# Turned identity transposes, first weights' low parts on GpSimd, and later or earlier low halves in a one-core transformer block

## The chip, the cores and the metric

The kernel runs on one core of one Trainium2 chip. TensorE (PE) multiplies matrices; its weight loads (PEld) run beside the products. VectorE (DVE), ScalarE (ACT) and GpSimd (POOL) do everything else on tiles, and SyncE (SP) issues nearly all transfers. Each engine works through its own instructions in a fixed order and stops at an instruction whose semaphore is not there yet. The metric is the device time of one execution in microseconds, taken as the median over several executions.

## The reference

One layer of a bidirectional hybrid encoder on x of 1024 tokens by 1024 features, in float32. What is computed:

```
h = rmsnorm(x, norm_mix);  proj = h @ w_in      # q k v r, low-rank decays, pool input, two gates
o = gla_forward(q,k,v,decay_f) + gla_backward(q,k,v,decay_b)   # 4 heads, chunked linear attention
y_a = (rmsnorm_per_head(o) * gla_norm * silu(r)) @ w_branch
y_b = (multiscale_pool(u) per group @ w_pool_group) * pool_scale
x = x + (sigmoid(g_a)*y_a + sigmoid(g_b)*y_b) @ w_out
x = x + (silu(gate) * up) @ w_ffn_out,  [gate | up] = rmsnorm(x, norm_ffn) @ w_ffn_in
return rmsnorm(x, norm_final)
```

The chunked attention keeps a state per head: for a chunk, `kv = k^T v`, and the state is `decay * state + kv`; the output of a chunk is a product of masked scores with v and a product of q with the state before the chunk.

## The kernel before

**Products in two halves.** Every float32 operand of a large product is split into a high half, a rounding to fp32r by a cast, mostly on ACT, and a low half, the rest, by a subtraction on DVE or POOL (`split_to`, L197 to L199). Three products take the place of one: high by high, high by low, low by high (`products`, `mm3`). A high half must exist before its low half can be made, so each split is a step of ACT followed by a step of DVE or POOL, and PE can start on the first of the three products before the low halves are there. Large products of the later stages are cut into Strassen-like seven-product schemes, whose sums and differences of blocks (`sub`, `add` on DVE, `padd` on POOL) come ahead of the splits.

**What sets the order.** The program is written out in order by generators. `mm3` calls `pump`, which after a given amount of PE work takes the next step of a side generator (`begin(gen, delay)`), so that transposes, norms and splits are interleaved with the running products. Each engine's order is fixed by that.

**The start** (L446 to L490). Rows of x come in eight tiles of 128 tokens. For each, ACT squares and sums it (`xn<-x`, L331), DVE adds the epsilon (`n1rs`, L322), POOL takes the power -1/2 (L323), DVE scales (`xn`, L327). PE transposes the scaled tile with `ident` (`tr`, L338), two tiles to a bank pair, ACT multiplies by the gain and casts (`hh`, L345), DVE makes the low half (`hl`, L348). PE forms the values of head 0 and the low-rank decays for one tile after the other (`first_values`, 288 columns, t = 0 to 7); their weights `raw` and `lraw` are split into `fwh` and `fwl` (L198, L199, L249, L251). ACT evicts each result (`vh`, `lr`) and DVE makes `vl`.

**A GLA head.** The backward scan runs over chunks 7 to 1. A step multiplies keys and values (`kv`), DVE makes the new state `st` (L764) and its decayed form `so` (L769), and ACT writes the state for later use into `sb` (L815). Between the steps PE transposes keys (`kp`, L750), which ACT and DVE split into `kt`, and forms the scores `sc` (L777), which DVE masks (L782) and which are split into `p`. Then the forward scan forms the output `op`: scores by values, and `sb` by q (L849).

**Merge and output product.** `merged_piece` (L1184) makes the operands of the seven products with `w_out`; for p = 6 it calls `sub`, `padd`, `sub` (L1198 to L1200), and the low half `dl` follows (L163).

**FFN operands.** `features(half)` (L1491) transposes the normalised rows; ACT evicts them into `hb` (L1506), DVE forms sums and differences (L1518, L1522), ACT casts them to `gh` (L1484), DVE makes the low half `gl` (L1488, `low_block`).

## Time and profile before

| | |
|---|---|
| median of 3 runs | 1383.6 us (1383.58 to 1387.52) |
| profiled execution | 1385.57 us |
| its span, first to last instruction | 1383.8 us |
| PE busy | 1362.2 us, 98% |
| DVE, POOL, ACT busy | 848.3, 757.6, 625.1 us |
| mean granted TensorE clock | 0.999 |

The span and the profiled execution's own time differ by 1.8 us, which lie around the span. A product of 512 columns starts every 0.23 us, one of 288 columns about every 0.14 us and one of 256 columns every 0.12 us; the durations of the rows are longer than that since products overlap. PE is busy for nearly the whole span, so the other engines matter where PE waits for them, and the table of waits names those places.

### The profile page before, as it was taken

The page shows a single profiled execution, that of the slowest core. Times are in us where ns is not written, and L with a number is a line of the kernel's source. Part 1 is how long each engine was busy: PE and PEld are TensorE (multiplying, and loading weights), DVE is VectorE, ACT ScalarE, POOL GpSimd, SP SyncE. Part 2 cuts the span into 40 slices and gives each one's busy share as a digit, 9 for nine tenths or more (in the row PEclk, how much of TensorE's full clock was granted, in tenths as well). Part 3 has the DMA queues.
Part 4 walks back from the last instruction along what each step waited for, and adds up shares of the span by engine and source line. Part 5 has one row for each costly group of instructions (what it writes and reads, how often), then busy time and mean ns, then how long its engine had stood idle before and what let it go on. Part 6 is the DMA issues. An engine that isn't in the chain of part 4 may idle for free.

```text
span 1383.8 us, 18503 instructions
## 1 busy us (share of the span) xinstructions
PE 1362.2 (98%) x6654; PEld 1150.9 (83%) x6654; DVE 848.3 (61%) x1073; ACT 625.1 (45%) x1125; POOL 757.6 (55%) x565
## 2 busy tenths in 40 slices
PE   7999999999999999999999999999999999999997
PEld 7889898988888877788888788888888888888886
DVE  6276767766645885587884856555655556343374
ACT  7365655644334444554346533333333334453252
POOL 3260715312398456568665276666666667464354
PEclk9999999999999999999999999999999999999999
DMA  6221322321487669997416355555444447975451
GB/s 193 77 92 44 110 82 87 122 77 46 138 264 238 211 198 310 334 393 257 152 61 240 118 175 175 175 175 175 159 141 141 145 137 267 385 256 216 167 232 73
DMA packets 167452, 243.56 MB, mean 176 GB/s; under 512 B 10904, under 2 KB 97856, under 8 KB 167360
## 3 DMA queue, kind: packets, MB, share of 16 engines
q1 hardware_dynamic: 154368, 215.11, 46.7%
q10 hardware_dynamic: 12992, 27.27, 5.3%
q8 instruction: 52, 0.85, 0.3%
q14 instruction: 40, 0.33, 0.1%
HBM read 164.48 MB, written 77.86 MB: 175 GB/s over the span
## 4 chain that ended last, share of the span: by engine, by line
PE 81%; POOL 5%; issue 4%; DVE 4%; ACT 3%; DMA 2%; ACTq 0%; POOLq 0%; SPq 0%; DVEq 0%
PE ps L291 75%; POOL wl L199 2%; PE op L849 2%; DMA u_out<-uph 1%; PE kv L291 1%; PE sc L777 1%; PE op L291 1%; POOL qe L733 1%; DVE res L1796 1%; POOL wsum L637 1%; PE yb L291 1%; PE tp L1008 1%; DMA u_out<-upl 0%; DMA raw<-in_w_in_dram 0%; DVE ws L1068 0%
## 5 line engine op out<-in xcount | busy, mean ns | idle before, releaser
L199 POOL TENSOR_TENSOR wl<-fs,wh 128x512 fp32r<-128x512 f32 x120 | 166.2, 1389 | 163.9 <-ACT wh L198 139.4
L291 PE MATMUL ps<-gl,wh 128*128 128x512 f32 x616 | 239.8, 389 | 0.9 <-DVE gl L1488 0.9
L291 PE MATMUL ps<-gh,wh 128*128 128x512 f32 x616 | 240.4, 390 | 0.0
L291 PE MATMUL ps<-gh,wl 128*128 128x512 f32 x616 | 239.7, 389 | 0.0
L199 POOL TENSOR_TENSOR wl<-fraw,wh 128x512 fp32r<-128x512 f32 x90 | 130.1, 1445 | 64.3 <-ACT wh L198 59.5
L199 POOL TENSOR_TENSOR wl<-raw,wh 128x512 fp32r<-128x512 f32 x44 | 63.8, 1463 | 159.0 <-ACT wh L198 158.9
L199 POOL TENSOR_TENSOR ol<-gor,oh 128x1024 fp32r<-128x1024 f32 (+1 forms) x42 | 99.8, 2382 | 92.3 <-ACT oh L198 71.8
L291 PE MATMUL ps<-hh,wh 128*128 128x512 f32 x376 | 149.8, 398 | 0.0
L291 PE MATMUL ps<-hh,wl 128*128 128x512 f32 x376 | 146.6, 390 | 0.0
L291 PE MATMUL ps<-hl,wh 128*128 128x512 f32 x376 | 146.5, 390 | 0.0
L291 PEld LDWEIGHTS ps<-gl,wh 128*128 128x128 f32 x616 | 115.7, 188 | 25.1 <-DVE gl L1488 1.3
L291 PEld LDWEIGHTS ps<-gh,wl 128*128 128x128 f32 x616 | 115.6, 188 | 24.0
L291 PEld LDWEIGHTS ps<-gh,wh 128*128 128x128 f32 x616 | 115.7, 188 | 23.6
L291 PE MATMUL ps<-ol,oh 128*128 128x512 f32 x308 | 119.9, 389 | 0.2 <-DVE ol L199 0.2
L291 PE MATMUL ps<-oh,oh 128*128 128x512 f32 x308 | 119.8, 389 | 0.0
L291 PE MATMUL ps<-oh,ol 128*128 128x512 f32 x308 | 119.8, 389 | 0.0
L199 POOL TENSOR_TENSOR wl<-wraw,wh 128x512 fp32r<-128x512 f32 x56 | 91.3, 1659 | 46.0 <-ACT wh L198 46.0
L199 DVE TENSOR_TENSOR ol<-wor,oh 128x1024 fp32r<-128x1024 f32 (+1 forms) x41 | 61.4, 1520 | 49.5 <-ACT oh L198 49.3
L198 ACT CAST wh<-fs 128x512 fp32r<-128x512 f32 x120 | 73.8, 615 | 32.1 <-DVE fs L918 23.8
L291 PEld LDWEIGHTS ps<-hh,wl 128*128 128x128 f32 x376 | 70.6, 188 | 15.0
L291 PEld LDWEIGHTS ps<-hl,wh 128*128 128x128 f32 x376 | 70.7, 188 | 13.2
L291 PEld LDWEIGHTS ps<-hh,wh 128*128 128x128 f32 x376 | 70.7, 188 | 13.2
(262 smaller groups left out, 3176.4 us busy)
## 6 DMA issues: line engine op xcount, KB each, us to landing
fraw<-in_w_ffn_in_dram SPq DMA_DIRECT2D x44, 512.0 KB, 6.2
gor<-g_out SPq DMA_DIRECT2D x35, 512.0 KB, 7.1
raw<-in_w_in_dram SPq DMA_DIRECT2D x48, 256.0 KB, 3.8
g_out<-s SPq DMA_DIRECT2D x44, 256.0 KB, 2.3
fraw<-in_w_in_dram SPq DMA_DIRECT2D x20, 512.0 KB, 4.5
wor<-t_out SPq DMA_DIRECT2D x20, 512.0 KB, 7.6
g_out<-g SPq DMA_DIRECT2D x33, 256.0 KB, 2.6
x<-in_x_dram SPq DMA_DIRECT2D x16, 512.0 KB, 4.3
```

Source lines behind the costliest of these rows:

```text
L198: nc.scalar.copy(hi, src)
L199: eng.tensor_tensor(lo, src, as_f32(hi), op=ALU.subtract)
L291: nc.tensor.matmul(ps, a[i], b[j], start=first and n == 0, stop=last and n == 2, skip_group_check=onto)
L637: op()
L733: nc.gpsimd.tensor_tensor(e_q[:, d, :], e_q[:, d, :], q[:, half, :], op=ALU.mult)
L777: nc.tensor.matmul(sc[d][:, i * CH : (i + 1) * CH], chunk_of(ke, n, d), chunk_of(qe, n, d), start=True, stop=True,)
L849: nc.tensor.matmul(op[:, :DV], a, b, start=False, stop=j == len(terms) - 1)
L1008: nc.tensor.transpose(tp[:, i * P : (i + 1) * P], o_heads[j // 2][half][:, i, (j % 2) * P : (j % 2 + 1) * P], ident[:, :],)
L1796: nc.vector.scalar_tensor_tensor(res[:, COLS[j]], x2[t][:, COLS[j]], rs[:, :], gain_final[:, COLS[j]], op0=ALU.mult, op1=ALU.mult)
```

## The change

The change has seven parts.

1. Before the first rows arrive, PE transposes `ident` 30 times into a bank that is never read (`spin(30)`), and 8 times more between the transposes of the first and the second row tile.
2. The four casts of `lraw` go from POOL to ACT, between the squares of tiles 0 and 1. The four subtractions that make `fwl` from `raw` are all on POOL; two of them were on DVE.
3. In `first_values` for t = 0 the products with low weights of the last four k-tiles come last.
4. The squares of tiles 2 and 3 are both taken before either is scaled. The transposes of these tiles come at the end of the product t = 1 rather than inside it. The square of tile 4 is taken early, its scaling later; the square of tile 5 comes after the evictions of t = 1.
5. In each GLA head the low halves of the first scores `p` and of the keys `kt` of the forward scan's first half are held back until the next state has been made, and the transposes of these keys come one step earlier.
6. `padd` in `merged_piece` becomes `add`, so this sum goes from POOL to DVE.
7. The low blocks of the fifth FFN product are made two transposes after their cast rather than three.

```diff
@@ -241,12 +241,15 @@
             self.todo = tiles
             self.parts = [tuple(slot(F32R, (2, VL), s) for s in ("fwh", "fwl")) for _ in tiles]
 
-        def split_values(self, i, eng):
-            split_to(*(t[:, :, :DV] for t in self.parts[i]), self.todo[i][:, :, :], eng)
+        def split_values(self, i):
+            hi, lo = (t[:, :, :DV] for t in self.parts[i])
+            src = self.todo[i][:, :, :]
+            nc.scalar.copy(hi, src)
+            nc.gpsimd.tensor_tensor(lo, src, as_f32(hi), op=ALU.subtract)
 
         def split_low(self):
             for i, (hi, _) in enumerate(self.parts):
-                nc.gpsimd.tensor_copy(hi[:, :, DV:], self.low[:, 2 * i : 2 * i + 2, :])
+                nc.scalar.copy(hi[:, :, DV:], self.low[:, 2 * i : 2 * i + 2, :])
             for i, (hi, lo) in enumerate(self.parts):
                 nc.gpsimd.tensor_tensor(
                     lo[:, :, DV:], self.low[:, 2 * i : 2 * i + 2, :], as_f32(hi[:, :, DV:]), op=ALU.subtract
@@ -392,13 +395,17 @@
 
     def norm_x(t):
         rs = norm_scale(xt[t % 4][:, :], xn[t % 4], "n1")
-        scale_by(xn[t % 4], xt[t % 4][:, :], rs)
-        if t + 4 < NT:
-            load_x(t + 4)
+
+        def scaled():
+            scale_by(xn[t % 4], xt[t % 4][:, :], rs)
+            if t + 4 < NT:
+                load_x(t + 4)
+
+        return scaled
 
     def norms(t0):
         for t in (t0, t0 + 1):
-            norm_x(t)
+            norm_x(t)()
             yield 2
 
     def values(w, v, t):
@@ -415,8 +422,20 @@
     def first_values(w, v, t):
 
         ps = bank(ps_mm)
-        for kt in range(KT):
-            mm3(ps[:, :VL], tokens(hT(kt, t // 4), t), w(kt), kt == 0, kt == KT - 1)
+        if t:
+            for kt in range(KT):
+                mm3(ps[:, :VL], tokens(hT(kt, t // 4), t), w(kt), kt == 0, kt == KT - 1)
+        else:
+            terms = [(kt, i, 0) for kt in range(KT) for i in range(2)]
+            for kt in range(4):
+                terms.insert(3 * kt + 1, (kt, 0, 1))
+            terms += [(kt, 0, 1) for kt in range(4, KT)]
+            for n, (kt, i, j) in enumerate(terms, 1):
+                nc.tensor.matmul(
+                    ps[:, :VL], tokens(hT(kt, 0), 0)[i], w(kt)[j], start=n == 1, stop=n == len(terms)
+                )
+                if n % 3 == 0:
+                    pump(VL / HALF)
         hi, lo = (part[:, t % 4, :] for part in v[t // 4])
         nc.scalar.copy(hi, ps[:, :DV])
         nc.scalar.copy(low_rows[:, t, :, :], ps[:, DV:VL].unsqueeze(1).broadcast_to([P, 4, 2 * RANK]))
@@ -440,8 +459,16 @@
     def value_slots():
         return [(slot(F32R, (4, DV), "vh"), slot(F32R, (4, DV), "vl")) for _ in range(2)]
 
+    def spin(n):
+        for _ in range(n):
+            nc.tensor.transpose(spun[:, :P], ident[:, :], ident[:, :])
+
+    spun = bank(ps_mm, "spun")
+    spin(30)
     v = value_slots()
-    norm_x(0)
+    norm_x(0)()
+    w = FirstWeights(first_raw, lraw)
+    w.split_low()
 
     vps = bank(ps_g, "vps")
     cols = [const.tile([P, n], F32, tag=f"cols{n}", name=f"cols{n}") for n in (8, n_rows)]
@@ -455,21 +482,35 @@
     g_mix = cols[0]
     g_ffn, g_gla, g_pool = (cols[1][:, 8 * i : 8 * i + 8] for i in range(3))
     b_dec = (cols[1][:, 24:28], cols[1][:, 28:32])
-    norm_x(1)
+    norm_x(1)()
     trs = [bank(ps_g, "tr") for _ in range(KT // 2)]
     for t in range(2):
         for kp, ps in enumerate(trs):
             transpose_tile(ps, xn[t], t, kp)
-    w = FirstWeights(first_raw, lraw)
-    w.split_low()
+        if t == 0:
+            spin(8)
     for i in range(KT // 2):
-        w.split_values(i, nc.vector if i < 2 else nc.gpsimd)
+        w.split_values(i)
     for kp, ps in enumerate(trs):
         gain_and_split(ps, kp, 0, hT, g_mix)
-    norm_x(2)
-    norm_x(3)
+    for scaled in [norm_x(t) for t in (2, 3)]:
+        scaled()
+    fifth = []
+
+    def fifth_mean():
+        fifth.append(norm_x(4))
+        yield 1
+
+    def fifth_and_sixth():
+        fifth.pop()()
+        yield 0.1
+        norm_x(5)()
+        yield 0.1
+
     for t in range(0, NT, 2):
-        if t + 4 < NT:
+        if t == 0:
+            begin(fifth_mean(), 1)
+        elif t + 4 < NT:
             begin(norms(t + 4), 1)
         if t == 2:
             for d, w_up in enumerate((w_decay_up_fwd, w_decay_up_bwd)):
@@ -481,7 +522,9 @@
         if t == 0:
             vectors(1, 8)
         if t + 2 < NT:
-            begin(to_features(xn[(t + 2) % 4 :], t + 2, hT, g_mix, 1 if t else 0.6), 0.5 if t else 2.2)
+            begin(to_features(xn[(t + 2) % 4 :], t + 2, hT, g_mix, 1 if t else 0.15), 0.5 if t else 3.9)
+        if t == 0:
+            begin(fifth_and_sixth())
         first_values(w, v, t + 1)
         finish_side()
         if t == 4:
@@ -744,12 +787,20 @@
         def chunk_of(e, n, d):
             return e[n // 4][:, d, (n % 4) * CH : (n % 4 + 1) * CH]
 
-        def transposed_keys(half, d):
+        def split_with(lows, hi, lo, src):
+            nc.scalar.copy(hi, src)
+            low = partial(nc.vector.tensor_tensor, lo, src, as_f32(hi), op=ALU.subtract)
+            if lows is None:
+                low()
+            else:
+                lows.append(low)
+
+        def transposed_keys(half, d, lows=None):
             kp = bank(ps_g, "kp")
             for i in range(4):
                 nc.tensor.transpose(kp[:, i * P : (i + 1) * P], chunk_of(ke, 4 * half + i, d), ident[:, :])
             kt = slot(F32R, s="kt")
-            split_to(kt[:, 0, :], kt[:, 1, :], kp[:, :])
+            split_with(lows, kt[:, 0, :], kt[:, 1, :], kp[:, :])
             return kt
 
         def advance(old, n, d, kt):
@@ -769,7 +820,7 @@
             nc.vector.tensor_scalar(old[:, :], new, factor(following, d, "whole"), None, op0=ALU.mult)
             return new, old
 
-        def scores(half):
+        def scores(half, lows=None):
             sc = [bank(ps_g, "sc") for _ in range(2)]
             for d in range(2):
                 for i in range(4):
@@ -780,7 +831,7 @@
                     )
             hi, lo = (t2(dtype=F32R, s="p")[:, :] for _ in range(2))
             nc.vector.copy_predicated(sc[1][:, :], keep.rearrange("p n c -> p (n c)"), sc[0][:, :])
-            split_to(hi, lo, sc[1][:, :])
+            split_with(lows, hi, lo, sc[1][:, :])
             return hi, lo
 
         sums(1, 1)
@@ -809,12 +860,15 @@
 
         sb = [slot(shape=(4, DV), s="sb") for _ in range(2)]
         old = None
+        lows = []
         for n in range(NT - 1, 0, -1):
             state, old = advance(old, n, 1, kts[n // 4, 1])
             m = n - 1
             nc.scalar.activation(
                 sb[m // 4][:, m % 4, :], state, AF.Copy, scale=factor(m, 1, "before")
             )
+            while lows:
+                lows.pop()()
             if n == 7:
                 yield 0.7
                 apply_decay(1, 0)
@@ -823,10 +877,10 @@
                 kts[0, 1] = transposed_keys(0, 1)
                 yield 0.5
             if n == 4:
-                p = scores(0)
+                p = scores(0, lows)
                 yield 2
-            if n == 2:
-                kts[0, 0] = transposed_keys(0, 0)
+            if n == 3:
+                kts[0, 0] = transposed_keys(0, 0, lows)
                 yield 0.5
         yield 1.2
         o = [slot(shape=(4, DV), s="o") for _ in range(2)]
@@ -1196,7 +1250,7 @@
             if p == 6:
                 s3s.append(slot(s="s3"))
                 sub(s3s[c][:, :, :], block(0, 0), block(1, 0))
-                padd(block(1, 0), block(1, 0), block(1, 1))
+                add(block(1, 0), block(1, 0), block(1, 1))
                 sub(block(0, 0), block(1, 0), block(0, 0))
             elif p == 3:
                 sub(block(0, 1), block(0, 1), block(0, 0))
@@ -1507,6 +1561,8 @@
                 blocks[k // 4, half][k % 4 // 2][:, k % 2, :], ps[:, :], AF.Copy, scale=g_ffn[:, k : k + 1]
             )
             i = k % 4 // 2
+            if half and k in (2, 4):
+                low_block(5, k // 2 - 1, block(0, 0, k // 2 - 1))
             if k % 2 and half == 0:
                 p, src = (1, block(0, 0, i)) if k < 4 else (2, block(1, 0, i))
                 cast_block(p, i, src)
@@ -1518,7 +1574,6 @@
                     sub(t, block(0, 1, i), t)
                     cast_block(5, i, t)
                 else:
-                    low_block(5, i, t)
                     sub(t, block(1, 1, i), t)
                     cast_block(6, i, t)
             yield 2 if half == 0 else 2.5 if k % 2 else 1
```

**ACT at the start, around the square of tile 5.** Rows of ACT before; the four squares `xn_132` to `xn_131` are tiles 2, 3, 4 and 5:

```order
L331 ACTIVATE xn_132,n1ms_252<-x_128 128x1024
L331 ACTIVATE xn_133,n1ms_259<-x_129 128x1024
L331 ACTIVATE xn_130,n1ms_273<-x_126 128x1024
L331 ACTIVATE xn_131,n1ms_291<-x_127 128x1024
L421 CAST vh_161<-ps_266 128x256
L422 COPY lr_158<-ps_266 128x128
L345 ACTIVATE hh_228<-tr_321,cols_173 128x256 x2
L345 ACTIVATE hh_234<-tr_333,cols_173 128x256 x2
L345 ACTIVATE hh_240<-tr_348,cols_173 128x256 x2
L345 ACTIVATE hh_246<-tr_360,cols_173 128x256 x2
L421 CAST vh_161<-ps_308 128x256
L422 COPY lr_158<-ps_308 128x128
```

The same engine and place in the change:

```order
L334 ACTIVATE xn_132,n1ms_291<-x_128 128x1024
L334 ACTIVATE xn_133,n1ms_296<-x_129 128x1024
L334 ACTIVATE xn_130,n1ms_312<-x_126 128x1024
L440 CAST vh_192<-ps_305 128x256
L441 COPY lr_158<-ps_305 128x128
L348 ACTIVATE hh_267<-tr_362,cols_220 128x256 x2
L348 ACTIVATE hh_273<-tr_374,cols_220 128x256 x2
L348 ACTIVATE hh_279<-tr_383,cols_220 128x256 x2
L348 ACTIVATE hh_285<-tr_392,cols_220 128x256 x2
L440 CAST vh_192<-ps_340 128x256
L441 COPY lr_158<-ps_340 128x128
L334 ACTIVATE xn_131,n1ms_405<-x_127 128x1024
```

The square of tile 5, `xn_131`, moved from ahead of the first eviction to behind eight gain casts and the second eviction.

**DVE in head 0, between the mask of the scores and the last states of the backward scan.** Before:

```order
L782 COPY_PREDICATED sc_1184<-keep,sc_1183 128x512
L199 TENSOR_TENSOR p_1194<-sc_1184,p_1193 128x512
L764 SCALAR_TENSOR_TENSOR st_1216<-kv_1212,fac_987,so_1168 128x256
L769 TENSOR_SCALAR so_1218<-st_1216,fac_987 128x256
L764 SCALAR_TENSOR_TENSOR st_1231<-kv_1227,fac_987,so_1218 128x256
L769 TENSOR_SCALAR so_1233<-st_1231,fac_987 128x256
L199 TENSOR_TENSOR vl_1050<-ps_1176,vh_1049 128x256
L199 TENSOR_TENSOR kt_1253<-kp_1248,kt_1253 128x512
L764 SCALAR_TENSOR_TENSOR st_1263<-kv_1259,fac_987,so_1233 128x256
```

The same place in the change:

```order
L833 COPY_PREDICATED sc_1223<-keep,sc_1222 128x512
L815 SCALAR_TENSOR_TENSOR st_1254<-kv_1250,fac_1026,so_1207 128x256
L820 TENSOR_SCALAR so_1256<-st_1254,fac_1026 128x256
L871 TENSOR_TENSOR p_1233<-sc_1223,p_1232 128x512
L199 TENSOR_TENSOR vl_1089<-ps_1215,vh_1088 128x256
L815 SCALAR_TENSOR_TENSOR st_1283<-kv_1279,fac_1026,so_1256 128x256
L820 TENSOR_SCALAR so_1285<-st_1283,fac_1026 128x256
L871 TENSOR_TENSOR kt_1271<-kp_1266,kt_1271 128x512
L815 SCALAR_TENSOR_TENSOR st_1302<-kv_1298,fac_1026,so_1285 128x256
```

The low half of `p` moved behind the first state; `vl` stands one state earlier, and the low half of `kt` still stands ahead of the last state, `st_1302`.

**DVE in `features(1)`, around the low blocks of the fifth and sixth products.** Before; `gl_7462` and `gl_7497` belong to the fifth product, `gl_7523` to the sixth, and `g` (L1639) is a sum of the gates beside them:

```order
L1518 TENSOR_TENSOR hb_7184<-hb_7435,hb_7184 128x1024
L1639 TENSOR_TENSOR g_7373<-ps_7450,g_7373 128x512
L1518 TENSOR_TENSOR hb_7185<-hb_7436,hb_7185 128x1024
L1488 TENSOR_TENSOR gl_7462<-hb_7184,gh_7461 128x1024
L1522 TENSOR_TENSOR hb_7184<-hb_7437,hb_7184 128x1024
L1639 TENSOR_TENSOR g_7375<-ps_7485,g_7375 128x512
L1488 TENSOR_TENSOR gl_7497<-hb_7185,gh_7496 128x1024
L1522 TENSOR_TENSOR hb_7185<-hb_7438,hb_7185 128x1024
L1639 TENSOR_TENSOR g_7377<-ps_7531,g_7377 128x512
L1488 TENSOR_TENSOR gl_7523<-hb_7184,gh_7522 128x1024
```

The same place in the change:

```order
L1574 TENSOR_TENSOR hb_7223<-hb_7474,hb_7223 128x1024
L1542 TENSOR_TENSOR gl_7501<-hb_7223,gh_7500 128x1024
L1694 TENSOR_TENSOR g_7412<-ps_7489,g_7412 128x512
L1574 TENSOR_TENSOR hb_7224<-hb_7475,hb_7224 128x1024
L1542 TENSOR_TENSOR gl_7537<-hb_7224,gh_7536 128x1024
L1577 TENSOR_TENSOR hb_7223<-hb_7476,hb_7223 128x1024
L1694 TENSOR_TENSOR g_7414<-ps_7525,g_7414 128x512
L1577 TENSOR_TENSOR hb_7224<-hb_7477,hb_7224 128x1024
L1694 TENSOR_TENSOR g_7416<-ps_7571,g_7416 128x512
L1542 TENSOR_TENSOR gl_7563<-hb_7223,gh_7562 128x1024
```

The two low blocks of the fifth product each moved ahead of the next difference on DVE; the first low block of the sixth, now `gl_7563`, stands where it stood, behind the second difference L1577.

## The prediction

> **What bounds the kernel.** I read the first part of the page, then the table of what PE waits for, then the timelines of the engines in the three stretches that the change touches.
>
> ```profile
> span 1383.8 us, 18503 instructions
> ...
> PE 1362.2 (98%) x6654; PEld 1150.9 (83%) x6654; DVE 848.3 (61%) x1073; ACT 625.1 (45%) x1125; POOL 757.6 (55%) x565
> ```
>
> PE works for all but 1383.8 - 1362.2 = 21.6 us of the span. No product is added to it or taken from it, so the change can pay only where PE waits. These are the rows of the waits that bear on it:
>
> ```profile
> PE tr L338 <- DVE xn L327: 2.6, 2, 2.2
> PE ps L291 <- ACT ga L1281: 1.6, 1, 1.6
> PE ps L291 <- DVE ga L1286: 1.4, 2, 0.8
> PE ps L291 <- DVE gl L1488: 0.9, 1, 0.9
> PE op L849 <- ACT sb L815: 0.9, 2, 0.6
> PE ps L291 <- DVE dl L163: 0.7, 1, 0.7
> ```
>
> Columns are total, times and longest. `op`, `dl` and `gl` are aimed at by parts 5, 6 and 7: 2.5 us in all, and a little more with the restart behind each wait. The `ga` waits lie between the heads and the merge and are not touched.
>
> **Parts 1 to 4, the start.** First PE, then ACT, DVE and POOL (start, duration, what; in square brackets the idle time before and its releaser), and two pieces of the chain of waits:
>
> ```profile
> 7.63 1.97 PE L338 MATMUL tr<-ident,xn 128*128 128x128 f32 x8 [2.24 <-DVE xn L327]
> 9.91 1.97 PE L338 MATMUL tr<-ident,xn 128*128 128x128 f32 x8 [0.31 <-DVE xn L327]
> 11.53 0.59 PE L291 MATMUL ps<-fwh,hh 128*128 128x288 f32 x1
> ...
> 12.38 0.29 PE L291 MATMUL ps<-fwh,hh 128*128 128x288 f32 x1
> ...
> 14.92 0.40 PE L291 MATMUL ps<-fwl,hh 128*128 128x288 f32 x1 [0.19 <-POOL fwl L199]
> ...
> 15.96 0.40 PE L291 MATMUL ps<-fwh,hh 128*128 128x288 f32 x1
> ...
> 21.63 0.40 PE L291 MATMUL ps<-fwh,hl 128*128 128x288 f32 x1 [0.16 <-DVE hl L348]
> ```
>
> ```profile
> 21.63 3.58 PE ps L291 x25
> 25.20 0.44 PE tr L338 x4
> ```
>
> ```profile
> 10.63 3.03 ACT L345 ACTIVATE hh<-tr,cols 128x256 fp32r<-128x256 f32 x8
> ...
> 18.32 1.68 ACT L345 ACTIVATE hh<-tr,cols 128x256 fp32r<-128x256 f32 x4
> ...
> 21.97 0.37 ACT L421 CAST vh<-ps 128x256 fp32r<-128x256 f32 x1
> ...
> 22.38 1.09 ACT L331 ACTIVATE xn<-x 128x1024 f32<-128x1024 f32 x1
> ```
>
> ```profile
> 11.51 3.23 DVE L348 SCALAR_TENSOR_TENSOR hl<-tr,cols,hh 128x256 fp32r<-128x256 f32 x8 [0.37 <-ACT hh L345]
> ...
> 24.56 0.14 DVE L322 TENSOR_SCALAR n1rs<-n1ms 128x1 f32<-128x1 f32 x1
> 25.37 0.75 DVE L327 TENSOR_SCALAR xn<-x,n1rs 128x1024 f32<-128x1024 f32 x1 [0.66 <-POOL n1rs L323]
> ```
>
> ```profile
> 1.08 0.29 POOL masks.py:199 TENSOR_SCALAR_AFFINE_SELECT ident<-ident 128x128 f32<-128x128 f32 x1
> ...
> 12.31 2.55 POOL L199 TENSOR_TENSOR fwl<-raw,fwh 128x512 fp32r<-128x512 f32 x2
> ```
>
> The turned identity. `ident` is there at 1.08 + 0.29 = 1.4 us. Early transposes go at (11.53 - 9.91) / 8 = 0.20 us each; later four take 0.44 us, so 0.11. Thirty at 0.20 end at 1.4 + 6.0 = 7.4, just before the rows come at 7.63: no delay from these. What they may bring is the quick pace from the start. But `hh` begins at 10.63 with no idle time before it, so ACT sets it, not PE, and `hl` waits for `hh` to 11.51. If the pace is quick, the eight turns between the tiles cost 0.9 us, which fit in ahead of tile 1 (8 x 0.11 for tile 0 ends at 8.5, the turns at 9.4, rows at 9.91). So I put the turning at nothing. If the pace stays slow, tile 0 ends at 7.63 + 1.6 = 9.2 and the turns at 10.8; tile 1 starts 0.9 us later than 9.91, and the first `hh`, which needs the first pair of both tiles, waits 0.9 us. At the upper reading of the row, 1.97 / 8 = 0.25 us each, the turns run from 1.4 to 8.8, tile 0 to 10.8, the eight to 12.8: 2.9 us late. The granted clock's column shows full speed throughout these stretches, so the pace of the rows has to tell the state. The first product still took 0.59 us at 11.53, and at 12.38 the same form took 0.29. Products had run for 0.85 us by then, transposes since 7.63: the early transposes seem to count as work.
>
> The Trainium skill, "TensorE: Matmul & The Clock Gate", Part 4 on the PE-mode transpose, says otherwise: the clock gate's fast state "doesn't engage" for transposes, since they do not count as busy in the same way. By that rule the thirty-eight turns would all stay slow, the case of 0.9 us just worked out. The quick pace 0.85 us behind the first product does not agree with it.
>
> Low weights. All four `fwl` on POOL take 2.55 / 2 = 1.28 us each; they can begin when POOL is done with the second power, where its casts began before, at about 9.1, so the last ends near 14.2. The products with it now come behind `hl`, which ends at 11.51 + 3.23 = 14.74. Behind 14.74 stand five products (one with `hl`, four with low weights), as five stood behind 14.92. So tile 0 ends about 0.15 us earlier and t = 1 begins at 15.8 instead of 15.96. The casts of `lraw` on ACT fit into its idle time ahead of the second square.
>
> Tiles 2 to 5. Up to the first transposes of t = 3 stand 51 products and four groups of transposes: 51 x 3.58 / 25 + 4 x 0.44 = 9.1 us. Without the wait at 21.63 PE is there at 15.8 + 9.1 = 24.9, against 25.20. But it needs tile 5 in that group. The first group for tiles 2 and 3 comes behind 21 products, at 15.8 + 3.0 = 18.8, and ends at 19.25. Then on ACT eight `hh` at 1.68 / 4 = 0.42 us (3.4), the evictions (22.38 - 21.97 = 0.4) and the square (1.1): 24.15. On DVE `hl` starts 0.9 us behind `hh` as before (11.51 - 10.63) and ends at 20.15 + 3.23 = 23.4; the scaling of tile 4 takes it to 24.1 and `vl` to 24.5. Then `n1rs`, the power and the scaling, 25.37 + 0.75 - 24.56 = 1.56: tile 5 is ready at 26.0. Its transposes came in the second half of the group, at 25.4; now at about 26.0. So PE, 0.3 us ahead, waits, and the start ends 0.6 us later than before. This wait `tr <- xn` is new. Unless DVE takes tile 5 sooner, the gain of parts 1 to 4 is lost here. Bounds: -0.3 (no wait) and +0.6 at the quick pace, +1.5 at 0.20 us, +3.5 at 0.25. I take +0.5.
>
> **Part 5, the heads.** Head 0, where PE waits three times:
>
> ```profile
> 107.38 0.38 PE L291 MATMUL kv<-vh,kt 128*128 128x256 f32 x1 [0.25 <-ACT kt L198]
> ...
> 108.11 0.38 PE L291 MATMUL kv<-vh,kt 128*128 128x256 f32 x1 [0.22 <-DVE kt L199]
> 109.04 0.70 PE L849 MATMUL op<-sb,qe 128*128 128x256 f32 x2 [0.55 <-ACT sb L815]
> ```
>
> ```profile
> 103.98 0.69 DVE L199 TENSOR_TENSOR p<-sc,p 128x512 fp32r<-128x512 f32 x1 [0.65 <-ACT p L198]
> 104.59 0.48 DVE L764 SCALAR_TENSOR_TENSOR st<-kv,fac,so 128x256 f32<-128x256 f32 x1
> ...
> 106.88 0.43 DVE L199 TENSOR_TENSOR vl<-ps,vh 128x256 fp32r<-128x256 f32 x1 [0.45 <-ACT vh L198]
> 107.36 0.69 DVE L199 TENSOR_TENSOR kt<-kp,kt 128x512 fp32r<-128x512 f32 x1
> 107.97 0.47 DVE L764 SCALAR_TENSOR_TENSOR st<-kv,fac,so 128x256 f32<-128x256 f32 x1
> ```
>
> DVE idles 0.65 us for the high half of `p`, then makes the low half, and the state `st` stands behind both. In the change this state can start at 103.98 - 0.65 = 103.33. From the first of these states to the last it took 107.97 - 104.59 = 3.38, of which 0.45 was idle; now it has the low `p` inside (104.59 - 103.98 = 0.61): 3.38 - 0.45 + 0.61 = 3.54. The last state starts at 106.9, or up to 0.3 us later if `vl` still waits for ACT. `op` followed it by 109.04 - 107.97 = 1.07, so it can run at 107.9 to 108.2 instead of 109.04: 0.8 to 1.1 us, and the two waits for `kt` lie ahead of that and vanish with it. PE would reach `op` at 109.04 - 1.02 = 108.0 or a little sooner, so a wait of 0.2 to 0.4 for `sb` can be left. I take -1.0. The other `op` wait of the table, 0.9 - 0.6 = 0.3 us in head 2, has the same form, and there the keys now come one step sooner: -0.3. The low half of `p` is needed behind 106.5 by the first `op` and is there by about 105, so nothing new waits for it. Bounds for all heads: -0.6, the low `p` alone, and -1.65, all waits with their restarts. I take -1.3.
>
> **Part 6, the merge.**
>
> ```profile
> 679.97 2.39 POOL L1199 TENSOR_TENSOR mg<-mg,mg 128x1024 f32<-128x1024 f32 x1 [1.16 <-DVE s L1198]
> ```
>
> ```profile
> 682.39 1.23 DVE L1200 TENSOR_TENSOR mg<-mg,mg 128x1024 f32<-128x1024 f32 x1 [2.50 <-POOL mg L1199]
> ```
>
> ```profile
> 684.81 0.50 PE L291 MATMUL ps<-wh,dl 128*128 128x512 f32 x1 [0.72 <-DVE dl L163]
> ```
>
> POOL takes 2.39 us for the sum while DVE idles 2.50. On DVE the same shape takes 1.23, so `mg`, its cast and `dl` come about 1.2 us sooner, more than the 0.72 us that PE waits. The whole wait goes, with the restart 0.9 us. DVE's added 2 x 1.23 us fall into its own idle time. Bounds -0.7 and -1.0; I take -0.9.
>
> **Part 7, the fifth and sixth products of the FFN.**
>
> ```profile
> 765.46 0.50 PE L291 MATMUL ps<-gl,wh 128*128 128x512 f32 x1 [0.87 <-DVE gl L1488]
> ```
>
> ```profile
> 766.47 1.22 DVE L1522 TENSOR_TENSOR hb<-hb,hb 128x1024 f32<-128x1024 f32 x1 [1.07 <-ACT hb L1506]
> ...
> 768.22 3.48 DVE L1488 TENSOR_TENSOR gl<-hb,gh 128x1024 fp32r<-128x1024 f32 x3
> ```
>
> The wait of 0.87 us for the fifth product's second `gl` goes. But eighteen products later, at 765.46 + 18 x 0.23 = 769.6, PE takes the first `gl` of the sixth product. That one is DVE's at 768.22 to 769.4, behind the difference at 766.47, which waited for ACT and not for the `gl` that moved. PE would now be there near 768.6 and wait to 769.45. The wait moves eighteen products on, and 0.2 us is gained. Bounds 0 and -1.0, if ACT and DVE come forward after all; I take -0.2.
>
> **The sum.** +0.5 - 1.3 - 0.9 - 0.2 = -1.9 us. The profiled execution took 1385.57 us (its span 1383.8, and 1.8 around it), so it would take 1383.7. It lies 2.0 above the median of 1383.6; that median would become 1381.7. One measurement tells about 0.3%, 4.15 us, from no change, so I forecast no change that can be told.
>
> **The rivals.**
> - Nothing is late next: PE passes tile 5 without waiting and ACT brings the sixth product forward: -0.3 - 1.65 - 1.0 - 1.0 = -3.95, 1379.6 us. For it speaks that ACT has idle time in the middle stretches; against it the queue of eight `hh` ahead of the square. Chance 0.14.
> - The turned transposes run at 0.20 us throughout and hold tile 1 back: +1.5 in place of +0.5, 1382.7 us. For it: PE is in order, and the sixteen early transposes stay at that pace in their rows. Against it: the quick pace soon behind. Chance 0.12. The Trainium skill's rule, named above, would give this case.
> - Slower: the same turning at the upper price of 0.25 us, +3.5, -2.4 elsewhere: +1.1, 1384.7 us. Tile 1 starts at 1.4 + 46 x p for a turn of p, so it decides from a lateness of 1.8 us, at p = 0.22. Against it: at that price the eight transposes from 9.91 would have ended at 11.9, and the first product stands at 11.53. Chance 0.06.
> - What the heads bring is swallowed: PE comes to the `ga` waits 1.3 us sooner and stands there longer, since these end by ACT and DVE: -0.6, 1383.0 us. Against it: what fills `ga` comes from PE's own earlier products and moves forward with them. Chance 0.10.
>
> **How the numbers follow.** The forecast has 0.58, with its own range from 1380.6 to 1382.9. The cases reach from 1379.6 to 1384.7; I take 1379.0 to 1384.4, the lower end for a little more at the start. Faster by over 0.3% lies below 1379.4: most of half of the first rival and the forecast's tail, 0.12. Slower by over 0.3% lies above 1387.7, which no case reaches; a run of 1387.52 stands among those shown, so 0.04. The rest, 0.84, is no change.
>
> **What would show it.** Right: `sb`, `kt`, `dl` are gone or below 0.4 us among PE's waits; `gl` is still there at 0.6 to 0.9, now at the sixth product; a new wait `tr <- xn` of 0.8 to 1.4 us near 25; the fifth tile's transposes no later than 0.8 us behind 25.4. Transposes at 0.27 us a row for tile 1 show the quick pace, 0.42 the slow. Wrong: the first product later than 11.6, or no wait near 25, or `gl` gone altogether.

## The result

The changed kernel takes 1382.4 us (median of 22 runs, 1380.76 to 1386.22), the kernel before 1384.55 us on the same chips (22 runs). The ratio is 0.9982, with a 95% interval from 0.9976 to 0.9989: 2.5 us less, between 1.5 and 3.3. Forecast were 1.9 us less and a change too small to tell from none; with 22 runs it can be told. The profiled execution took 1382.99 us, its span is 1381.3 against 1383.8. So the sum came out. By the profiled executions two of its terms did not, and they nearly cancel each other, which is luck.

PE's waits after the change:

```profile
PE ps L294 <- ACT ga L1335: 1.4, 1, 1.4
PE spun L464 <- POOL ident masks.py:199: 1.4, 1, 1.4
PE tr L341 <- DVE xn L330: 1.4, 2, 1.1
PE tr L341 <- DVE n1rs L325: 1.2, 1, 1.2
PE ps L294 <- DVE gl L1542: 0.8, 1, 0.8
PE op L903 <- ACT sb L867: 0.4, 1, 0.4
PE ps L434 <- DVE hl L351: 0.4, 1, 0.4
```

`dl` and both `kt` waits are gone and `op` is down to 0.4 us, as forecast. `gl` is still there at 0.8, as forecast. The forecast wait `tr <- xn` near 25 us is there too: it is the row `tr <- n1rs` with 1.2, since PE moves on at 27.57, when DVE's scaling of that tile (26.77 to 27.52) is done. Not forecast: the `ga` waits were 3.0 us in three pieces and are 1.4 in one.

Where the time went shows best when the start of one and the same PE instruction is taken from both timelines and subtracted (the turns left out). Positive is later than before; the marks are times of the kernel before.

| profiled execution | tile 1 | 25 us, tile 5 | 289 us, heads done | 480 | 600 | 690 | 1000 |
|---|---|---|---|---|---|---|---|
| changed kernel | +0.76 | +2.31 | +0.88 | +0.76 | -1.42 | -2.47 | -2.52 |
| parts 5 to 7 alone | +0.29 | +0.26 | -1.51 | -1.63 | -1.22 | -2.27 | -2.33 |
| parts 1 to 4 alone | +1.57 | +2.67 | +2.54 | +2.51 | -0.73 | -0.77 | -0.74 |
| two `fwl` on DVE | +0.18 | +1.50 | -0.25 | -0.38 | -1.93 | -2.98 | -3.04 |
| no turns | +1.83 | +3.69 | +2.33 | +2.21 | +1.64 | +0.59 | +0.57 |
| delay in the start | +1.55 | +2.62 | +3.40 | +3.35 | +0.72 | -0.33 | -0.35 |
| delay in the merge | +1.89 | +2.41 | +1.09 | +1.13 | -0.51 | +0.65 | +0.58 |
| sixth `gl` sooner | +0.73 | +1.25 | -0.09 | -0.21 | -2.38 | -3.43 | -4.24 |
| more turns | +1.24 | +1.76 | +0.42 | +0.49 | -2.74 | -3.79 | -3.87 |
| parts 5 to 7, delay | -0.26 | -0.24 | +0.13 | +0.01 | -2.43 | -3.49 | -3.56 |
| square of tile 5 early | +1.51 | +2.07 | +0.71 | +0.78 | -2.39 | -3.44 | -3.51 |
| light start | -0.10 | -0.22 | -1.96 | -1.87 | -2.88 | -3.93 | -4.74 |
| its control, without it | +0.47 | +0.76 | -1.05 | -1.01 | -2.11 | -3.17 | -3.95 |

Read along the first row: the start loses 2.3 us, the heads bring 1.4 back, the stretch from 480 to 600 us, where the `ga` waits lie, brings 2.2, the merge 1.05, the FFN 0.05.

Each row is one execution against one of the kernel before, and two things limit what it tells. The four executions with the old start (the kernel before, parts 5 to 7 alone, the same with the delay, the control of the light start) stand at tile 5 between -0.24 and +0.76, so a difference of up to 1 us in the start need not be a kernel's own. And the profiled execution of the kernel before took 1385.57 us, 1.0 above the median of its 22 runs; all rows share what it lost. Some of that can lie in the `ga` stretch: its last `ga` wait ended at 555.2 us, and in three kernels that came to 480 us within 0.4 us of it (two `fwl` on DVE, sixth `gl` sooner, parts 5 to 7 with the delay) at 552.8 to 553.3.

The start in the changed kernel's timelines, PE, DVE and POOL:

```profile
7.63 1.09 PE L341 MATMUL tr<-ident,xn 128*128 128x128 f32 x8 [0.32 <-DVE xn L330]
8.56 1.04 PE L464 MATMUL spun<-ident 128*128 128x128 f32 x8
10.67 1.09 PE L341 MATMUL tr<-ident,xn 128*128 128x128 f32 x8 [1.08 <-DVE xn L330]
11.67 0.40 PE L434 MATMUL ps<-fwh,hh 128*128 128x288 f32 x1
...
12.56 0.40 PE L434 MATMUL ps<-fwh,hl 128*128 128x288 f32 x1 [0.35 <-DVE hl L351]
...
27.57 0.44 PE L341 MATMUL tr<-ident,xn 128*128 128x128 f32 x2 [1.19 <-DVE n1rs L325]
```

```profile
8.86 1.76 DVE L330 TENSOR_SCALAR xn<-x,n1rs 128x1024 f32<-128x1024 f32 x1 [0.83 <-POOL n1rs L326]
12.02 3.23 DVE L351 SCALAR_TENSOR_TENSOR hl<-tr,cols,hh 128x256 fp32r<-128x256 f32 x8 [1.40 <-ACT hh L348]
```

```profile
8.80 5.43 POOL L248 TENSOR_TENSOR fwl<-raw,fwh 128x512 fp32r<-128x512 f32 x4
```

The turning did bring the quick pace: the sixteen transposes take 1.09 us per eight instead of 1.97. But the scaling of tile 1, 0.75 us before, takes 1.76. It starts 0.06 us behind the first `fwl` that POOL now makes in that place. Tile 1 comes at 10.67 instead of 9.91, and PE stands idle for 1.08 us. Then the granted clock falls. Four windows of the changed kernel's start follow; the number in brackets behind PE's busy time counts the transposes and products that run in the window, and the clock is the column behind POOL:

```profile
1.50:5.50 4.00, 4.00 (x19) 4.00 (x20) 2.80 (x6) 1.39 (x2) 2.26 (x31) 1.00 0.95 247
6.20:6.90 0.70, 0.70 (x9) 0.70 (x7) 0.13 (x1) 0.43 (x3) 0.70 (x2) 1.00 1.07 360
13.20:15.80 2.60, 2.60 (x12) 2.60 (x12) 2.20 (x7) 2.60 (x6) 1.35 (x2) 0.50 0.44 181
18.00:20.00 2.00, 2.00 (x18) 2.00 (x17) 0.80 (x4) 0.00 (x0) 0.55 (x1) 1.00 0.92 233
```

Between 13.2 and 15.8 us the clock is 0.50 and 12 products run. In the kernel with the sixth `gl` sooner, whose start is the same program, the same window reads:

```profile
13.20:15.80 2.60, 2.60 (x18) 2.23 (x18) 2.17 (x7) 2.60 (x6) 1.35 (x2) 1.00 0.49 183
```

There 18 products run at 1.00. The two executions differ by 1.06 us at tile 5. So the fall is not in every execution. Of the six profiled executions with eight turns and POOL's `fwl`, the clock fell in four (the changed kernel, parts 1 to 4 alone, the delay in the start, the early square) and held in two (the delay in the merge, the sixth `gl` sooner). PE's idle time ahead of tile 1 does not decide it: it was 1.08 to 2.11 us in the four, and 2.22 and 1.08 us in the two. They do differ in when the turns became quick: by the starts of the single turns at 5.3 to 6.1 us in the four, at 4.8 and 4.4 us in the two. Whether that decides it was not tested.

### The profile page after: what moved, and what is told of

The parts are those of the page before. It is cut to its first block, busy times and chain, and to the rows that moved or that the text cites. A ratio compares the mean times of both kernels' runs of the same rounds, so it can differ in the third digit from the quotient of the medians.

```text
span 1381.3 us, 18581 instructions
## 1 busy us (share of the span) xinstructions
PE 1366.6 (99%) x6692; PEld 1156.7 (84%) x6692; DVE 852.5 (62%) x1073; ACT 625.6 (45%) x1129; POOL 755.2 (55%) x561
## 4 chain that ended last, share of the span: by engine, by line
PE 91%; DVE 2%; POOL 2%; issue 2%; ACT 2%; DMA 2%; ACTq 0%; POOLq 0%; DVEq 0%; SPq 0%
PE ps L294 83%; PE op L903 2%; PE kv L294 1%; PE sc L828 1%; DMA u_out<-uph 1%; PE op L294 1%; DVE res L1851 1%; DMA fraw<-in_w_ffn_in_dram 1%; PE yb L294 1%; PE tp L1062 1%; PE kp L801 0%; POOL wl L199 0%; POOL wsum L680 0%; PE tr L341 0%; POOL qe L776 0%
## 5 line engine op out<-in xcount | busy, mean ns | idle before, releaser
L294 PEld LDWEIGHTS ps<-hh,wh 128*128 128x128 f32 x376 | 70.7, 188 | 13.2
```

What stands on the lines that cost most here:

```text
L294: nc.tensor.matmul(ps, a[i], b[j], start=first and n == 0, stop=last and n == 2, skip_group_check=onto)
```

## The experiments

Each kernel ran in turn with the kernel before; ratios are to that one. Two theories stood first. Theory A: what PE loses in the start is lost at the end. Theory B: the `ga` waits take it in.

**Parts 5 to 7 alone**, and **parts 1 to 4 alone**. The first is the kernel before with the three later parts, the second the changed kernel without them.

> Parts 5, 6 and 7 alone; the start is that of the kernel before. Seen in the changed kernel's trace: heads -1.4, merge -0.9, FFN -0.3 us. Theory A (what PE loses at the start is still lost at the end): 2.6 us below before plus what the ga waits happen to give, that is -2.5 to -4.5 us, and clearly below the changed kernel. Theory B (the ga waits end on transfers and take in whatever PE lost or gained ahead of them): only what lies behind them counts, -1.2 us, and the ga waits grow by 1 to 1.4 us against before.

> Parts 1 to 4 alone; heads, merge and FFN as before. Theory A: PE is 2.3 us late at the tile 5 transposes and the kernel ends 1 to 2.3 us later than before. Theory B: same lateness at 27 us, but the ga waits shrink by as much and the end is within 0.5 us of before.

Measured: 1382.02 us, ratio 0.9984 (0.9974 to 0.9994), for parts 5 to 7; 1384.93 us, 1.0003 (0.9994 to 1.0012), for parts 1 to 4. So parts 5 to 7 bring 2.2 us (0.8 to 3.6) by themselves, and the start brings nothing: its cost is 0.4 us, between -0.8 and +1.7. By the traces the start's lateness of 2.67 us at tile 5 is all gone at 600 us, while parts 5 to 7 alone, 1.63 us early at 480 us, were still 1.22 us early at 600. Neither theory fits both traces; the intervals of the timed runs alone would leave room for either.

**The first two low parts on DVE again.**

```diff
-            nc.gpsimd.tensor_tensor(lo, src, as_f32(hi), op=ALU.subtract)
+            eng.tensor_tensor(lo, src, as_f32(hi), op=ALU.subtract)
-        w.split_values(i)
+        w.split_values(i, nc.vector if i < 2 else nc.gpsimd)
```

> The changed kernel with the first two fwl low parts on DVE again. If the scaling of tile 1 (1.76 us, was 0.75) was held by GpSimd's fwl on the same SBUF side, it takes 0.75 again and tile 1's transposes start at 9.9 instead of 10.67. If the fall of the clock to 0.5 (12.9 to 16.1 us) came from PE's idle time ahead of them, the clock stays at 1.0 or falls for less long. Then PE's lateness at the tile 5 transposes goes from +2.3 to +0.3..+0.8 us. End: theory A 1.5 to 2 us below the changed kernel, theory B no difference. If GpSimd was not the cause, the scaling stays at 1.7 us.

Measured: 1382.19 us, 0.9983 (0.9974 to 0.9992). DVE and POOL in its trace:

```profile
9.28 0.75 DVE L330 TENSOR_SCALAR xn<-x,n1rs 128x1024 f32<-128x1024 f32 x1 [0.67 <-POOL n1rs L326]
9.95 2.37 DVE L248 TENSOR_TENSOR fwl<-raw,fwh 128x512 fp32r<-128x512 f32 x2
```

```profile
10.28 3.18 POOL L248 TENSOR_TENSOR fwl<-raw,fwh 128x512 fp32r<-128x512 f32 x2 [1.03 <-ACT fwh L247]
```

With POOL idle, the scaling of tile 1 takes 0.75 us, and in each of the eight traces here with POOL's `fwl` beside it, it takes 1.75 or 1.76: POOL holds it up. But now DVE's two `fwl` run against POOL's two and take 2.37 us instead of 1.36 before, so `hl` is late and PE still 1.50 us late at tile 5, where 0.3 to 0.8 was expected. The clock held at 1.00 in this execution. In the timed runs it is the changed kernel's time.

The Trainium skill, "SBUF — State Buffer", section "SBUF: two separate sides", says that DVE and GpSimd share one pair of ports as an exclusive lock, held for a whole instruction, for DVE work in a two-port mode or with two inputs from SBUF. The 1.76 and 0.75 us agree with it. So do the first two of POOL's four rows in the changed kernel, taken singly:

```profile
8.80 1.27 POOL L248 TENSOR_TENSOR fwl<-raw,fwh 128x512 fp32r<-128x512 f32 x1
```

```profile
10.03 1.72 POOL L248 TENSOR_TENSOR fwl<-raw,fwh 128x512 fp32r<-128x512 f32 x1
```

The first subtraction, begun 0.06 us ahead of the scaling, is not slowed. The scaling ends 0.55 us behind it, at 10.62, and the second subtraction takes 1.72 us where the last two take 1.28 each.

**Without the turns.** Both calls of `spin` and the bank are removed.

> The changed kernel without the 38 turns of the identity. If the turning only moved the quick clock ahead into a time in which PE then idles, the start is not later than with it: transposes at 0.2 us each as before, the clock rises near 12 to 13 us and stays, lateness at tile 5 +0.8 to +1.6 us (the scaling of tile 1 still takes 1.76). If the turning helps, lateness is +2.3 or more. End: theory A 0.5 to 1.5 us below the changed kernel, theory B no difference.

Measured: 1384.13 us, 0.9996 (0.9987 to 1.0006): 1.9 us above the changed kernel by the ratios. The expectation of something faster fell: by these runs the turns help, though the two intervals still touch. In this trace the products run one every 0.24 us till 17.4 us, with the clock column at 1.00. Its first rows came late, so the 3.69 us at tile 5 is not all due to the turns: tile 1's scaling began at 9.94, and at 8.86 in the changed kernel.

**A delay in the start, and the same in the merge.** Twenty turns go into the bank of the product t = 7, or into the first bank of the products with `w_out`; the products overwrite them.

```diff
         ps = bank(ps_mm)
+        if t == 7:
+            for _ in range(20):
+                nc.tensor.transpose(ps[:, :P], ident[:, :], ident[:, :])
```

> The changed kernel, with 20 turns of the identity (20 x 0.11 = 2.2 us of PE) put ahead of the last product of the first stage (t = 7), behind all the waits of the start. Theory A (lateness ahead of the ga waits counts at the end): 2.0 to 2.2 us above the changed kernel. Theory B (the ga waits take it in): 0 to 0.7 us above it, and PE's wait for ga, 1.4 us in the changed kernel, is gone.

> The changed kernel with the same 20 turns put ahead of the first product with w_out, behind the ga waits. Both theories: 2.0 to 2.2 us above the changed kernel, since nothing behind waits for a transfer. It is the measure for the run before. If the wait for gl in the FFN takes part of it in, 1.4 us.

Measured: 1385.93 us, 1.0010 (1.0002 to 1.0019), and 1385.63 us, 1.0008 (0.9999 to 1.0017). By the ratios they are 3.9 and 3.6 us above the changed kernel; at the nearest ends of the intervals the first is still 1.8 above. The traces show 2.2 us for each at its place, and the wait for `ga` that theory B has vanish stays at 0.9 us. The delay in the start costs as much as the one behind the `ga` waits, so theory B falls: from where the changed kernel stands, later is later. Why it is 1.4 to 1.7 us more than 2.2 is left open; the intervals reach down to 2.2.

**The sixth product's first low block sooner.**

```diff
+            elif half and k == 6:
+                low_block(6, 0, block(0, 0, 0))
...
         for i in range(2):
             cast_block(3, i, block(1, 1, i))
-            low_block(6, i, block(0, 0, i))
+            if i:
+                low_block(6, i, block(0, 0, i))
```

> The changed kernel with the first low block of the sixth FFN product taken ahead of the second difference (two transposes behind its cast, as the fifth's are). If the wait for gl moved from the fifth to the sixth product because DVE had that difference in front, it is gone now and the kernel is 0.6 to 0.8 us below the changed one. If ACT's cast was the late part, nothing changes.

Measured: 1381.98 us, 0.9980 (0.9972 to 0.9989), 0.3 us below the changed kernel, less than the interval. The trace is clear: there is no `gl` wait, and between 690 and 1000 us it gains 0.81 where the changed kernel gains 0.05. The changed kernel's own rows, PE and DVE:

```profile
767.04 0.50 PE L294 MATMUL ps<-gl,wh 128*128 128x512 f32 x1 [0.78 <-DVE gl L1542]
```

```profile
764.02 1.23 DVE L1577 TENSOR_TENSOR hb<-hb,hb 128x1024 f32<-128x1024 f32 x1 [2.20 <-ACT hb L1560]
765.16 0.68 DVE L1694 TENSOR_TENSOR g<-ps,g 128x512 f32<-128x512 f32 x1
765.76 2.35 DVE L1542 TENSOR_TENSOR gl<-hb,gh 128x1024 fp32r<-128x1024 f32 x2
```

The `gl` of 765.76 stood behind the difference of 764.02, for which DVE had idled 2.20 us.

**More turns between the tiles.** `spin(22)` in place of `spin(8)`.

> The changed kernel with 22 turns between the first two row tiles in place of 8, which keep PE busy till about 10.3 us. If the clock fell to 0.5 (12.9 to 16.1 us) because PE stood idle from 9.6 to 10.7, it does not fall now and PE's lateness at the tile 5 transposes goes from +2.3 to +1.0..+1.5 us; the scaling of tile 1 stays at 1.76 us. If turns do not count for the clock, it falls all the same. At the end 0 to 1 us below the changed kernel.

Measured: 1382.6 us, 0.9991 (0.9982 to 1.0000): no gain that can be told, where up to 1 us was expected; by the ratios it is 1.2 us above the changed kernel. In the trace the clock is 1.00 in every window from 4 to 18 us; but two of the six executions with eight turns kept it too, so this alone does not show that the idle time makes it fall. The turns became quick at 4.9 us in it, near the two that kept the clock. Its lateness at tile 5, 1.76 us, is more than the 1.0 to 1.5 expected. Relative to before, tile 5 was 0.52 us later than tile 1 had been.

**Parts 5 to 7 with the delay.** After the results above a third theory: the `ga` waits take in the first 2 us of lateness and no more.

> Parts 5, 6 and 7 with the start of before, and the 20 turns (2.2 us of PE) ahead of the last product of the first stage. In the traces so far the four kernels with a late start lost 1.6 to 3.2 us of it again in the ga stage (480 to 600 us), the one with the start of before nothing. Theory C (the ga waits take in the first 2 us of lateness and no more): 0 to 0.8 us above the kernel with parts 5 to 7 alone, and PE's ga waits down from 3.3 to about 1.5 us. Theory A (lateness counts in full): 2.0 to 2.5 us above it, ga waits unchanged at about 3 us.

Measured: 1383.49 us, 0.9985 (0.9976 to 0.9994), against 0.9984 without the delay. By the ratios the 2.2 us cost 0.1 us, give or take 1.9, so a full 2.2 lies just outside. The waits for `ga` in the kernel with parts 5 to 7 alone, from PE's timeline, and in the one with the delay, from its table of waits:

```profile
496.41 0.50 PE L291 MATMUL ps<-trh,wh 128*128 128x512 f32 x1 [0.95 <-DVE ga L1297]
...
540.94 0.50 PE L291 MATMUL ps<-trh,wh 128*128 128x512 f32 x1 [1.20 <-DVE ga L1297]
```

```profile
PE ps L291 <- ACT ga L1295: 1.0, 1, 1.0
```

Early on, PE waits twice for DVE's `ga` and once, 1.2 us, for ACT's; 2.2 us later, not at all for DVE's and 1.0 us for ACT's. The stretch from 480 to 600 us gives 2.4 us back. So theory C fits these two kernels, the two delays and parts 1 to 4 alone. It doesn't fit all: without the turns PE was 2.2 us late and got back 0.6. And four kernels that were early at 480 us, by 0.21 to 1.87, gained another 1.0 to 2.2 there, while parts 5 to 7 alone lost 0.4. Each row is one execution, and what ends these waits is a chain with transfers in it. ACT's rows ahead of its last `ga` wait, in the kernel before and in the changed one:

```profile
553.58 0.62 ACT L629 CAST uph<-fraw 128x512 fp32r<-128x512 f32 x1 [4.82 <-DMA u_out<-uph]
...
554.60 0.59 ACT L1281 COPY ga<-ps 128x512 f32<-128x512 f32 x1 [0.40 <-ACT uph L629]
```

```profile
552.19 0.62 ACT L672 CAST uph<-fraw 128x512 fp32r<-128x512 f32 x1 [4.65 <-DMA u_out<-uph]
...
553.21 0.59 ACT L1335 COPY ga<-ps 128x512 f32<-128x512 f32 x1 [0.40 <-ACT uph L672]
```

ACT takes its instructions in order, so the copy into `ga` stands behind a cast that waits 4.82 or 4.65 us for a transfer. The eight kernels that were late at 480 us got back 0.6 to 3.2 us. That lateness is paid back there in part is what these traces and the timed runs of parts 1 to 4 alone and of parts 5 to 7 with the delay speak for; the delay in the changed kernel's start, which cost its full length, speaks against a fixed amount. How much is paid back, and by what rule, was not settled.

**The square of tile 5 early.** It is taken with that of tile 4, as before the change.

> The changed kernel with the square of tile 5 taken early again, with that of tile 4 and ahead of the first eviction. If the late square is what holds the tile 5 transposes, as the prediction has it, its n1rs and power no longer stand between the vl eviction and the scaling: the transposes come 0.8 us sooner, PE's lateness there goes from about +2.2 (seen: +1.25 to +2.7 with this start) to about +1.4. If DVE's queue ahead (hl, scaling of tile 4, vl) sets it, it moves by 0.8 us at most and the wait tr <- xn stays. At the end -0.8 us against the changed kernel if it counts, 0 if not.

Measured: 1382.27 us, 0.9980 (0.9970 to 0.9991), as the changed kernel. PE's row at tile 5:

```profile
27.33 0.44 PE L341 MATMUL tr<-ident,xn 128*128 128x128 f32 x2 [0.38 <-DVE n1rs L325]
```

The wait is 0.38 us instead of 1.19: 0.8 less, as expected. So the late square did make that wait. The clock fell in this execution, which would explain why tile 5 is 0.56 us later than tile 1 all the same.

**A light start**, to beat both: parts 5 to 7, the sixth `gl` sooner, and of the start the turns (30, and 12 between the tiles) and the late products with low weights. Casts, low parts, squares and transposes of the start stay as before the change. **Its control** has the old start.

> Parts 5 to 7 with the sixth product's first low block sooner as well (-0.8), and of the start only the turns (30 and 12) and the low-weight products last; casts, low parts, squares and transposes of the start as before. If the parts of the start that cost time are the low parts on GpSimd and the late square, PE is at most 0.3 us later than before at the tile 5 transposes, and up to 0.5 sooner; the end is 1.0 to 1.5 us below parts 5 to 7 alone. If the turns themselves cost time, PE is 0.5 us late or more.

> The light-start kernel without its start: parts 5 to 7 and the sixth product's first low block sooner, start as before. If the turns and the late low-weight products bring something, this one is above the light-start kernel (1379.8, ratio to before 0.9959): a start 0.2 us earlier in the trace is worth 0.2 us, so 0.9961. If they bring more than PE's lateness shows, 1 us or more, 0.9967 or above. If they bring nothing, 0.996. From the trace of the parts: -2.3 - 0.8 = -3.1 us, 0.9978.

Measured: 1379.83 us (6 runs), 0.9959 (0.9944 to 0.9973), faster than both kernels, and by the ratios 3.5 us below parts 5 to 7 alone, where 1.0 to 1.5 was expected; the control 1382.03 us, 0.9978 (0.9969 to 0.9987). In the light start the scaling of tile 1 is 0.75 us again and PE passes tile 5 0.22 us earlier than before, with no wait there. The control has what the parts add up to, 2.3 + 0.8 = 3.1 us. The light start's surplus of 2.6 us over it is more than the 1.0 us that their traces differ by at tile 5; the intervals overlap by 0.0004 and leave room for that. Of the 1.0 us, 0.57 is there at tile 1, whose scaling began at 9.57 in the control and at 8.88 in the light start. The control's products also ran at the slow pace for long, one every 0.24 us till 15.6 us, with the clock column at 1.00:

```profile
13.20:15.80 2.60, 2.60 (x13) 2.60 (x13) 2.15 (x7) 2.60 (x6) 2.48 (x3) 1.00 0.71 265
```

In the three other executions with this start the quick pace came at 12.0 to 13.2 us. So without the turns it comes sooner or later from execution to execution; with them, in the nine traces that have them, it came at 4.4 to 6.1 us, ahead of the first row tile.

## Why the prediction was right, and where not

- **Heads, -1.3.** Right. From tile 5 to 289 us the changed kernel gains 1.43 us, and the eleven others with part 5 gain 1.3 to 1.8 (the delay taken off), parts 1 to 4 alone 0.13. The forecast wait of 0.2 to 0.4 us for `sb` is there with 0.4.
- **Merge, -0.9.** Right: 1.05 us in every kernel with part 6 (the delayed merge less its delay), 0.04 without. The restart was a little dearer than put.
- **FFN, -0.2.** Right in mechanism: the wait moved eighteen products on, and is 0.78 us there. It gained 0.05; taking it away brings 0.81.
- **The wait for tile 5.** Right: the new wait is there, and 0.8 us of it goes with the square put back. Where the clock held (delayed merge, sixth `gl` sooner, more turns), tile 5 was later than tile 1 had been by 0.52 us in each of the three. +0.5 had been taken for the whole start, so this term has its size. But the tile's transposes came at 27.57, 2.2 us behind 25.4, where at most 0.8 had been named as the sign of being right.
- **The start as a whole, +0.5, in the traces +1.2 to +2.7.** Three steps of the working failed, and one of the prediction's own signs of being wrong appeared: the first product came at 11.67, later than 11.6. First, that turns and casts leave tile 1 at 9.91: the low parts on POOL were costed by POOL's time, 1.28 us each, and by the deadline of their products, and not by what they hold up on DVE. The scaling went from 0.75 to 1.76 us; in the changed kernel tile 1 came 0.76 us late. Second, that the quick pace stays once it is there: the clock fell to 0.50 for about 3 us in the changed kernel, and 12 products ran there where 18 could have, which is 6 x 0.13 = 0.8 us in that window alone; behind tile 1, PE lost 1.55 us to tile 5 there, and 1.10 and 1.07 in two others whose clock fell (parts 1 to 4 alone, the delay in the start), against 0.52 with a clock that held. Third, the turning was put at nothing: without it the kernel is 1.9 us longer by the ratios, with intervals that touch.
- **No term for the `ga` waits.** They were named as not touched, and as a rival only in the other direction, that they swallow what is gained. Between 480 and 600 us PE got back 2.18 us against the one execution of the kernel before, of which up to about 1 us can be that execution's own. So the timed start of 0.4 us, near the forecast +0.5 though its trace is 2.67 us late, and with it the sum, came out by luck: a start that was worse than put, and a payback that was not put at all.

The forecast rivals with slow turns did not come: the thirty went at 0.21 us each till 6 us and at 0.11 from there, by the windows above (19 in 4.00 us, then about 7 in 0.70), after 4.6 us of nothing but transposes; in the other eight traces with the turns the change came between 4.4 and 6.1 us. The Trainium skill's Part 4 on the PE-mode transpose, in "TensorE: Matmul & The Clock Gate", has it that transposes do not raise the clock. Here the pace doubled with nothing but transposes running, and the measurement decides.

## What to carry to other kernels

Before work is moved to an engine with idle time, look at what the other engines do in those very microseconds: DVE's scaling more than doubled beside POOL's subtraction, though each engine's own row looked free. When a wait is removed, find the next instruction that needs the same engine's queue; here the gain of 0.8 us needed one more line. And when a kernel has waits that end on something other than PE, lateness ahead of them may be paid back in part, so judge an early stage by timed runs of the whole kernel, with a control of a known delay.

## What the runs showed of the hardware that was not expected

- The scaling of a 128x1024 tile on DVE takes 0.75 us alone and 1.75 to 1.76 beside POOL's subtraction of a 128x512 tile, in all eight traces with that pairing. Two subtractions on DVE took 1.36 us beside POOL's casts and 2.37 beside POOL's subtractions.
- Identity transposes alone raise PE's pace from 0.21 to 0.11 us a piece, between 4.4 and 6.1 us in the nine traces where they start at 1.4. In that stretch the clock column reads 1.00 for both paces, so it does not show the slow state before the first rise (nor in the control of the light start, where products ran one every 0.24 us till 15.6 us at 1.00); the later fall it does show, with 0.50.
- With the same start, the clock fell to 0.50 in four executions and held in two. PE had stood idle ahead of tile 1 for 1.08 to 2.11 us in the four and for 2.22 and 1.08 us in the two, so the length of that idle piece does not set it. By what it is set is open.
